# A four-layer diffusion backbone on one core: the first transfers in a fixed order, the latent stream first, and zero matmuls in idle places of TensorE

## The chip, the core and the metric

The kernel runs on one core of a Trainium2 chip. The engines of the core have their own instruction queues and run beside each other: TensorE (PE, with the loading of its weights shown apart as PEld), VectorE (DVE), ScalarE (ACT), GpSimd (POOL), and SyncE (SP), whose queue issues all transfers here. The metric is the time of one execution on the device in microseconds (us), as the median of several runs.

## The reference: what is computed

256 latent tokens and 256 context tokens, 1024 wide, go through four layers. Each layer has a token mixer (attention, pooling, retention, attention) and a SwiGLU feed-forward part (FFN), each behind an RMS norm that is modulated by a condition vector, with a gated residual. In the last layer the context stream has no output of its own.

```python
def pre_norm(xs, gain, shift, scale):
    return rmsnorm(xs, gain) * (1 + scale) + shift

def swiglu(h, w_gate, w_up, w_down):
    return (jax.nn.silu(h @ w_gate) * (h @ w_up)) @ w_down
...
    cond_lat = jax.nn.silu(c)[:, None, :]
    for i in range(DEPTH):
        sh_m, sc_m, g_m, sh_f, sc_f, g_f = jnp.split(cond_lat @ ada_w[i] + ada_b[i], 6, axis=-1)
        h_l = pre_norm(x_lat, norm_mix[i], sh_m, sc_m)
        ...                                  # the same for the context, with c_ctx
        x_lat = x_lat + g_m * y_l            # y_l: attention, pooling or retention
        x_lat = x_lat + g_f * swiglu(pre_norm(x_lat, norm_ffn[i], sh_f, sc_f),
                                     ffn_w_gate[i], ffn_w_up[i], ffn_w_down[i])
```

## The kernel before

**Data.** The activations stay on the chip, transposed: 128 partitions hold a block of features, KT = 8 such blocks (k) make the 1024, and the free axis holds 512 tokens, `STREAM[0]` the 256 latent and `STREAM[1]` the 256 context ones. Weights come from memory as 512 KB tiles `wall` (128x1024), modulation weights as tiles `adaw` of the same size. Products are exact to float32: each weight tile and each normed tile h is split into a rounded high part and the low rest (`w_prep`: ACT makes the high part with a CAST of 128x1024, DVE or POOL the low one with a subtraction of the same size; `norm2`: ACT and DVE or POOL make the parts of h), and three products are summed in PSUM, which has eight banks (`ps`, one 128x512 tile each).

**A norm.** `addsq` squares the stream's eight blocks (ACT) and sums them (DVE). `norm1` multiplies the sum by a column of ones on PE (128x1), takes the inverse root with a Newton iteration of some eight small DVE instructions, and puts it on a diagonal (two 128x128 DVE instructions). `norm2` spreads the diagonal over all partitions with a product against ones (two 128x128 on PE, "the spread" below), multiplies x by it and by the modulation (a DVE `SCALAR_TENSOR_TENSOR`), and writes h. In layers after the first this is called by `boundary`, which stands between two sub-layers: the latent stream is normed while the tail of the sub-layer before (`ctail`, on the context) still gives PE work, then the context, then the first products of the next sub-layer run. `boundary` in `pool` and in the FFN are two of its callers.

**The first layer.** `start` loads x, the first eight weight tiles and the modulation weights in pieces (`START`: 128, 128, 256 and 512 features, for scale and for shift), computes each piece's modulation on PE (32x128 matmuls, `ada_rows`), makes the h blocks that it allows, and runs the K and V products of the four token blocks (`kv`) as far as there is h. `consts` loads one table of small data (`small`: constants, rotary tables, the condition), and lets ACT compute silu of the condition.

**What sets the order.** The kernel is written as one sequence, recorded (`Recorder`), and laid out anew by a planner for the whole program: `schedule` tries priorities in several rounds, `attempt` gives each engine the ready instruction of the highest priority, with modelled costs, a bank of PSUM for each `ps` tile from its first to its last instruction, and data dependences as the only ties. So an edit in one place can move instructions in others. All instructions are emitted on one line (L550), so that rows of the profile name operation, tile and shape, not the place in the code.

Of the kernel before, what the change touches and what calls it, by code (L numbers as in the profile page):

```python
# [175 lines left out]
class Recorder:  # L176
# [23 lines left out]
    def record(self, eng, name, args, kw, calls=None):  # L200
# [59 lines left out]
        self.ops.append(op)  # L260

# [324 lines left out]
class Builder:  # L586
# [67 lines left out]

    def tr(self, out, in_):
        self.nc.tensor.transpose(out, in_, self.ident)
        self.clock += 0.109
# [98 lines left out]
    def consts(self):  # L756
        nc, cp, a = self.nc, self.cp, self.a
        sm = self.small = cp.tile([P, SM_END], F32, name="small", const=True)
        nc.sync.dma_start(sm, a["small"])
        x = self.xall = cp.tile([P, KT, 512], F32, name="x")  # L760
        self.x = [x[:, k, :] for k in range(KT)]
        self.ident = cp.tile([P, P], F32, name="ident", const=True)
# [10 lines left out]
        nc.scalar.activation(self.cond[:, :, 0:2], sm[:, SM_C:SM_END].rearrange("p (k c) -> p k c", c=2), AF.Silu)  # L773
        self.nsink = cp.tile([P, 32], F32, name="nsink", const=True)
# [43 lines left out]
    def norm1(self, s):  # L818
# [3 lines left out]
        for b in range(2):  # L822
            for i, t in enumerate(terms):
                self.mm(ps[:, b : b + 1], t[:, tb_cols(b)], self.inv_d, i == 0, i == len(terms) - 1)
        self.last[s] = []
# [7 lines left out]
    def norm2(self, s, A, B, ks=range(KT)):  # L833
# [3 lines left out]
        if ks[0] == 0:  # L837
            ps = self.ps()
            for b in range(2):
                self.mm(ps[:, tb_cols(b)], self.ones, self.dg[s][:, tb_cols(b)], True, True)  # L840
            self.rps[s] = ps
# [19 lines left out]
    def boundary(self, ctail, A, B, lhead, chead, ctx=True, fill=()):  # L861
# [139 lines left out]
    def ffn(self, l, ctail, ctx, bfill=(), fill=(), mid=None):  # L1001
# [52 lines left out]
        for half in range(2):  # L1054
            gs = []
            if half == 0:
# [12 lines left out]
                self.boundary(ctail, A, B, head(LAT), head(CTX), ctx, bfill)  # L1069
# [55 lines left out]
    def start(self, A, B, kv, setup):  # L1125
# [5 lines left out]
        def load_x(s):  # L1131
            for k in range(0, KT, 4):
                nc.sync.dma_start(self.xall[:, k : k + 4, STREAM[s]], self.a["xin"][s, :, k : k + 4, :])

        def load(c0, n, ci):
# [6 lines left out]
        load_x(0)  # L1142
        for i, p in enumerate(pieces):
            load(*p)
            if i == 1:
                load_x(1)
            if i % 2 and (p[0] + p[1]) % 256 == 0:
                self.w_dma()
        for s in range(2):
# [3 lines left out]
        gens = [kv(tb) for tb in range(4)]  # L1153
        for c0, n, ci in pieces:
# [19 lines left out]
            if ci == 0:  # L1174
                ks = range(c0 // P, (c0 + n) // P)
                for s in range(2):
                    self.norm2(s, A, B, ks)
                setup()
                for g in gens:
                    self.run(g, nq)  # L1180
        for g in gens:
            self.run(g)
# [53 lines left out]
    def attention(self, l, slot, ctail, need_ctx, bfill=(), fill=()):  # L1236
# [7 lines left out]
        self.adepth = 4  # L1244
        kvkeys = []
        for k in range(KT):
            for c in range(4):
                kvkeys.append(("attn_w_qkv", slot, ((k * P, P),), D + c * P))
# [29 lines left out]
        def kv(tb):  # L1278
            ps = self.ps()
            for k in range(KT):  # L1280
                self.mmR(ps, self.hx(k, tb_cols(tb)), self.blk(held[4 * k], 4), k == 0, k == KT - 1)
# [6 lines left out]
        def setup():  # L1288
            if not held:
                self.w_retire()  # L1290
                held.extend(self.take(kvkeys, True))
                KH.extend(self.slot(F32R) for _ in range(2))
# [8 lines left out]
        if l == 0:  # L1301
            self.start(A, B, kv, setup)
        else:
            self.boundary(ctail, A, B, head(0), head(1), True, bfill)
# [11 lines left out]
        def qgen(g):  # L1316
            qr = {}
            bs = self.take([("attn_w_qkv", slot, ((k * P, P),), g * 256 + c * P) for k in range(KT) for c in range(2)])
            for par in range(2):
                Q[g, par] = self.slot(F32R)  # L1320
# [20 lines left out]

            for tb in tbs:
# [685 lines left out]
```

## Time and profile before

| | us |
|---|---|
| median of 3 runs | 2198.64 (2198.44 to 2198.74) |
| profiled execution, its own time | 2198.0 |
| its span in the profile | 2196.2 |
| PE busy in the span | 2169.7 (99%) |
| weight loads on PE (PEld), beside its matmuls | 1826.2 (83%) |
| DVE busy | 1529.0 (70%) |
| ACT busy | 874.4 (40%) |
| POOL busy | 131.1 (6%) |

The profile is of one execution; 1.8 us of its time lie outside the span. PE has work nearly all the time, so the rows to read are those on the few stretches in which it has none, and on the clock it is granted: the clock column is 1.00 at the higher of its two levels (2.4 GHz) and 0.50 at the lower (1.2 GHz), and a mean of both lies between them.

### The profile page before, as it was taken

What the parts mean: (1) busy time and instruction counts of PE and PEld (TensorE: products, weight loads), DVE (VectorE), ACT (ScalarE), POOL (GpSimd) and SP (SyncE); (2) the same over time, 40 slices, a digit from 0 to 9 for tenths busy, and PEclk for the clock granted to TensorE, in tenths of its full rate; (3) what the DMA queues carried; (4) which work ended last, traced back from release to release, by engine and by line L of the source; (5) the groups of instructions that cost most, each with busy time, mean ns of one, the idle gap of its engine ahead of it and who ended that gap; (6) DMA issues with size and microseconds to landing.
All of it is one profiled execution on the core that took longest, in us unless ns stands there. A gap on an engine that the chain in (4) does not pass through costs nothing.

```text
span 2196.2 us, 29879 instructions
## 1 busy us (share of the span) xinstructions
PE 2169.7 (99%) x11378; PEld 1826.2 (83%) x11378; DVE 1529.0 (70%) x3075; ACT 874.4 (40%) x1529; POOL 131.1 (6%) x145
## 2 busy tenths in 40 slices
PE   8999999999999999999999999999999999999999
PEld 5787988888898888888888888889888888877888
DVE  5888867677598777766364554458677765898674
ACT  5587522223272222324332333335222223587552
POOL 2222000000010000000000000000000000441000
PEclk9999999999999999999999999999999999999999
DMA  9413545655235565532232232234456543125562
GB/s 380 164 36 105 183 145 171 227 165 185 75 131 196 182 232 180 169 119 82 73 97 90 77 96 77 82 110 159 158 163 220 172 143 116 49 87 192 163 203 85
DMA packets 88944, 315.27 MB, mean 144 GB/s; under 512 B 9824, under 2 KB 13024, under 8 KB 88800
## 3 DMA queue, kind: packets, MB, share of 16 engines
q1 hardware_dynamic: 88800, 313.36, 43.5%
q8 instruction: 89, 1.46, 0.3%
q14 instruction: 55, 0.45, 0.1%
HBM read 312.27 MB, written 1.05 MB: 143 GB/s over the span
## 4 chain that ended last, share of the span: by engine, by line
PE 95%; DVE 3%; DMA 1%; ACT 0%; issue 0%; SPq 0%; ACTq 0%; DVEq 0%
PE t L550 95%; DVE t L550 3%; ACT t L550 0%; DMA t<-wall 0%; DMA t<-xin 0%; ACT L550 0%; SPq L550 0%; ACTq L550 0%; DVEq L550 0%
## 5 line engine op out<-in xcount | busy, mean ns | idle before, releaser
L550 PE MATMUL t<-t,t 128*128 128x512 f32 (+5 forms) x11378 | 2169.7, 362 | 22.8 <-DVE t L550 18.7
L550 PEld LDWEIGHTS t<-t,t 128*128 128x128 f32 (+1 forms) x11378 | 1826.2, 185 | 366.0 <-issue 47.8
L550 DVE TENSOR_TENSOR t<-t,t 128x256 f32<-128x256 f32 (+7 forms) x1278 | 782.0, 642 | 395.2 <-ACT t L550 190.3
L550 ACT CAST t<-t 128x1024 fp32r<-128x1024 f32 (+3 forms) x646 | 526.5, 833 | 744.9 <-DVE t L550 343.3
L550 DVE SCALAR_TENSOR_TENSOR t<-t,t 128x1024 bf16<-128x1024 f32 (+5 forms) x472 | 400.4, 862 | 52.7 <-DMA t<-adaw 40.7
L550 ACT ACTIVATE t<-t 128x256 f32<-128x256 f32 (+4 forms) x357 | 160.7, 461 | 416.4 <-PE t L550 304.5
L550 DVE SCALAR_TENSOR_TENSOR t<-t,t,t 128x256 f32<-128x256 f32 (+2 forms) x500 | 229.4, 499 | 114.7 <-PE t L550 108.6
L550 POOL TENSOR_TENSOR t<-t,t 128x2 f32<-128x2 f32 (+5 forms) x124 | 127.5, 1038 | 1853.5 <-ACT t L550 1737.2
L550 ACT ACTIVATE t<-t,t 128x256 fp32r<-128x256 f32 (+2 forms) x180 | 89.2, 541 | 46.2 <-DVE t L550 45.4
L550 DVE TENSOR_REDUCE t<-t 128x1 f32<-128x512 f32 (+5 forms) x128 | 67.3, 551 | 16.0 <-PE t L550 14.9
L550 ACT COPY t<-t 128x256 f32<-128x256 f32 (+2 forms) x116 | 53.1, 469 | 56.4 <-PE t L550 52.5
L550 ACT ACTIVATE t<-t,t,t 128x512 f32<-128x512 f32 (+1 forms) x96 | 67.0, 706 | 19.7 <-DVE t L550 15.5
L550 DVE TENSOR_SCALAR t<-t 128x2 int32<-128x2 int32 (+4 forms) x84 | 16.1, 196 | 79.0 <-ACT t L550 71.6
L550 DVE TENSOR_SCALAR t<-t,t 128x512 f32<-128x512 f32 (+2 forms) x94 | 36.4, 419 | 1.0
L550 DVE DVE_READ_ACCUMULATOR t<-t,t 128x1 f32 x304 | 25.1, 82 | 0.0
L550 DVE COPY t<-t 128x512 f32<-128x512 f32 x32 | 21.8, 685 | 1.0 <-PE t L550 0.8
L550 ACT ACTIVATION_READ_ACCUMULATOR t<-t,t,t 128x1 f32 x96 | 19.3, 201 | 0.0
L550 DVE SCALAR_TENSOR_TENSOR t<-t 128x2 f32<-128x2 f32 (+1 forms) x94 | 15.6, 167 | 1.9
L550 ACT ACT_TABLE_LOAD x6 | 7.7, 1283 | 8.4 <-DVE t L550 5.7
L550 DVE TENSOR_TENSOR t<-t 128x2 f32<-128x2 f32 (+1 forms) x47 | 8.9, 192 | 0.9
L550 DVE RECIPROCAL t<-t 128x2 f32<-128x2 f32 (+1 forms) x40 | 6.4, 165 | 0.6
L550 ACT ACTIVATION_READ_ACCUMULATOR t<-t 128x1 f32 x32 | 6.3, 196 | 0.0
(9 smaller groups left out, 4.6 us busy)
## 6 DMA issues: line engine op xcount, KB each, us to landing
t<-wall SPq DMA_DIRECT2D x386, 512.0 KB, 3.7
t<-adaw SPq DMA_DIRECT2D x192, 512.0 KB, 4.6
t<-condw SPq DMA_DIRECT2D x6, 512.0 KB, 3.7
t<-xin SPq DMA_DIRECT2D x4, 512.0 KB, 5.9
t<-strips SPq DMA_DIRECT2D x4, 512.0 KB, 4.4
t<-pm SPq DMA_DIRECT2D x2, 512.0 KB, 4.1
out_dram<-t SPq DMA_DIRECT2D x8, 128.0 KB, 1.7
t<-small SPq DMA_DIRECT2D x1, 412.0 KB, 5.6
```

What stands on the lines that cost most here:

```text
L550: getattr(getattr(nc, op.eng), name)(*args, **kw)
```

## The change

- **Transfers.** `small` is loaded in three parts: condition first, then constants, the rotary tables last. A new `follow(a, b, ...)` records a tie between instructions, and the first ones of the queue are tied in this order: condition, two halves of the latent x, the first scale piece, constants, the first shift piece, a weight tile, the context x. The other pieces are loaded in groups.
- **First norm.** silu of the condition is ahead of the squares of the latent stream. Three of the eight latent squares are made by DVE. In the first layer the spread is copied from PSUM to a tile (`keep`) by ACT. The streams are interleaved as latent h, latent K and V, then context h, context K and V, in each piece; before, both streams' h came before the products.
- **Zeros.** `warm(count, n)` records matmuls of a bf16 tile of zeros with itself into a PSUM tile that nobody reads: 22 of 512 and 24 of 256 columns at the start, and 8 and 9 of 512 at two boundaries (`warm=True`): behind norm1 and behind the spread of the latent stream. The two callers are the FFN's boundary behind a mixer without context output (`not ctx`, layer 3) and the pooling layer's. The tie is only to what stands ahead of them; nothing waits for a zero.
- **Attention of layer 0.** `start` is called after the functions for q are defined; a part of `qgen` becomes `qfin`. `setup` makes the K and V tiles only when they are first needed.

```diff
+    def warm(self, count, n=512, after=None):
+        ps = self.ps()
+        for _ in range(count):
+            self.nc.tensor.matmul(
+                ps[:, 0:n], self.idle[:, 0:P], self.idle[:, 0:n], start=True, stop=True, skip_group_check=True
+            )
+            if after is not None:
+                self.nc.follow(after, self.nc.ops[-1])
...
-        nc.sync.dma_start(sm, a["small"])
+        for c0, c1 in ((SM_C, SM_END), (0, SM_PSC), (SM_PSC, SM_C)):
+            nc.sync.dma_start(sm[:, c0:c1], a["small"][:, c0:c1])
+            self.loads.append(nc.ops[-1])
...
+        nc.gpsimd.memset(self.idle, 0.0)
+        self.warm(22)
+        self.warm(24, 256)
...
+            if keep is not None:
+                nc.scalar.copy(keep[:, 0:256], ps[:, 0:256])
+                ps = keep
...
         self.norm1(0)
+        if warm:
+            self.warm(8, 512, self.normed)
         self.norm2(0, A, B)
+        if warm:
+            self.warm(9, 512, self.spread)
...
-                self.boundary(ctail, A, B, head(LAT), head(CTX), ctx, bfill)
+                self.boundary(ctail, A, B, head(LAT), head(CTX), ctx, bfill, not ctx)
...
+            for k in range(KT):
+                xs = self.x[k][:, LAT]
+                if k in (1, 3, 5):
+                    V.tensor_tensor(q[k], xs, xs, ALU.mult)
+                else:
+                    nc.scalar.activation(q[k], xs, AF.Square)
+                    if k == 0:
+                        nc.follow(self.silu, nc.ops[-1])
...
+        load_x(0)
+        load(*pieces[0])
+        line.append(self.loads[1])
+        load(*pieces[1])
+        self.w_dma()
+        line.append(nc.ops[-1])
+        load_x(1)
+        nc.follow(*line)
...
+        for i, (c0, n) in enumerate(START):
+            for ci in (2, 0):
+                modulation(c0, n, ci)
+            ks = range(c0 // P, (c0 + n) // P)
+            for s in range(2):
+                if i == 0 and s == 1:
+                    squares(1)
+                if i == 1 and s == 0:
+                    load_group(4)
+                self.norm2(s, A, B, ks, keep[s])
+                setup(False)
+                for g in streams[s]:
+                    self.run(g, n // P)
...
-        self.boundary(ctail, A, B, head(0), head(1), True, bfill)
+        self.boundary(ctail, A, B, head(0), head(1), True, bfill, True)
```

How the instructions stand on PE at the start of the program, before. The rows of 128x1 are norm1 of a stream, those of 32x128 a modulation block, those of 128x128 transposes and the spread, and the last is the first product (weights `t_274`, h `t_270`).

```order
L550 MATMUL t_167<-t_74,t_138 128x1
L550 MATMUL t_167<-t_74,t_156 128x1
...
L550 MATMUL t_191<-t_80,t_84 32x128 x8
L550 MATMUL t_210<-t_82,t_84 32x128 x8
...
L550 MATMUL t_231<-t_138,t_110 128x128
...
L550 MATMUL t_251<-t_87,t_84 32x128 x8
L550 MATMUL t_265<-t_74,t_174 128x1
...
L550 MATMUL t_288<-t_274,t_270 128x512
```

The same place after. `t_123` is the tile of zeros, `t_181` the latent norm1, `t_234` its spread, `t_283` the first product.

```order
L557 MATMUL t_134<-t_123 128x512
...
L557 MATMUL t_165<-t_79,t_74 32x128 x8
...
L557 MATMUL t_181<-t_84,t_148 128x1
...
L557 MATMUL t_186<-t_82,t_74 32x128 x8
...
L557 MATMUL t_234<-t_148,t_109 128x128 x2
...
L557 MATMUL t_242<-t_123 128x256
...
L557 MATMUL t_269<-t_89,t_74 32x128 x8
...
L557 MATMUL t_283<-t_219,t_275 128x512
```

Fourteen zeros now stand ahead of the first modulation block, one between it and norm1, seven more up to just behind the spread, and fourteen of 256 columns from there to the first product; the other ten of 256 columns stand among the first products. The context's norm1 (`t_265` of before) no longer stands ahead of the first product.

SP's queue from its first row on, before.

```order
L550 DMA t_72<-xin 128x4x256 x2
L550 DMA t_77<-small 128x824
L550 DMA t_72<-xin 128x4x256
L550 DMA t_80<-adaw 128x1024
L550 DMA t_82<-adaw 128x1024
L550 DMA t_72<-xin 128x4x256
L550 DMA t_87<-adaw 128x1024
L550 DMA t_89<-wall 128x1024
```

And after, with the rows of the last pieces of the first layer's modulation weights at the end (places 22 to 29).

```order
L557 DMA t_72<-small 128x16
L557 DMA t_76<-xin 128x4x256 x2
L557 DMA t_79<-adaw 128x1024
L557 DMA t_72<-small 128x256
L557 DMA t_82<-adaw 128x1024
L557 DMA t_86<-wall 128x1024
...
L557 DMA t_72<-small 128x552
...
L557 DMA t_132<-edge 128x64
L557 DMA t_179<-adaw 128x1024
L557 DMA t_193<-wall 128x1024
L557 DMA t_208<-adaw 128x1024
L557 DMA t_256<-adaw 128x1024
```

One weight tile (`t_86`) has moved ahead of the context x, `small` is in three pieces, and the last four modulation tiles of the first layer stand at places 26, 28, 29 and 33 of the queue, where before the last of them is at place 25.

PE at the boundary before the last FFN (layer 3), before: norm1 (`t_17921`), the spread (`t_17946`), and the first products of the FFN.

```order
L550 MATMUL t_17921<-t_74,t_138 128x1
L550 MATMUL t_17921<-t_74,t_17925 128x1
...
L550 MATMUL t_17946<-t_138,t_110 128x128 x2
L550 MATMUL t_17968<-t_17959,t_17775 128x512
L550 MATMUL t_17968<-t_17959,t_17790 128x256
L550 MATMUL t_17978<-t_17959,t_17620 128x512
```

And after.

```order
L557 MATMUL t_17992<-t_84,t_17994 128x1
...
L557 MATMUL t_18001<-t_123 128x512
...
L557 MATMUL t_18024<-t_148,t_109 128x128 x2
...
L557 MATMUL t_18031<-t_123 128x512
...
L557 MATMUL t_18056<-t_18044,t_17856 128x512
L557 MATMUL t_18056<-t_18044,t_17870 128x256
L557 MATMUL t_18062<-t_18044,t_17738 128x512
L557 MATMUL t_18062<-t_18044,t_17794 128x256
```

Eight zeros stand between norm1 and spread, nine between spread and first product, and four accumulations (`t_18056`, `t_18062`, `t_18067`, `t_18073`) now begin on the first h (`t_18044`).

The zeros recorded at the boundary of the pooling layer stand at two other places. On PE, after, around 630 us and in the attention of layer 3:

```order
L557 MATMUL t_6663<-t_249,t_109 128x128 x2
...
L557 MATMUL t_6669<-t_123 128x512
...
L557 MATMUL t_6685<-t_6455,t_5755 128x256
...
L557 MATMUL t_16749<-t_16368,t_16334 128x256
...
L557 MATMUL t_6669<-t_123 128x512
...
L557 MATMUL t_16854<-t_16622,t_16709 128x512
```

`t_6663` is the spread of the context at the boundary before the FFN of layer 1, with six zeros behind it; three more into the same tile `t_6669` stand some 5,800 rows later. Eight others (`t_6447`) stand before, behind the latent spread of the same boundary.

## Rows read from the trace of the kernel before

**Rows 1.** PE's waits, whole span: engine, line, released by: us, times, longest us

```profile
PE t L550 <- DVE t L550: 18.7, 10, 8.9
PE t L550 <- ACT t L550: 3.8, 6, 1.2
```

**Rows 2.** Windows: start:end length, busy us of each engine (instructions), clock, DMA share, GB/s

```profile
17.66:22.00 4.34, 4.29 (x33) 2.31 (x32) 3.94 (x18) 0.34 (x2) 0.00 (x0) 1.00 1.02 405
...
22.00:62.80 40.80, 40.62 (x282) 30.77 (x278) 25.83 (x65) 23.38 (x48) 22.51 (x16) 1.00 0.84 332
62.80:65.00 2.20, 0.07 (x1) 0.00 (x0) 2.20 (x22) 0.00 (x0) 0.00 (x0) 1.00 0.57 119
65.00:70.00 5.00, 4.95 (x32) 3.61 (x36) 4.43 (x13) 1.46 (x3) 1.43 (x2) 0.66 0.56 183
...
620.00:626.40 6.40, 5.68 (x33) 5.51 (x34) 4.84 (x23) 3.58 (x5) 0.00 (x0) 0.73 0.75 287
626.40:631.00 4.60, 2.39 (x17) 1.96 (x16) 4.60 (x14) 4.03 (x9) 0.73 (x1) 1.00 0.38 114
...
2006.50:2012.00 5.50, 5.45 (x16) 4.33 (x17) 5.42 (x11) 4.07 (x10) 3.41 (x4) 0.51 0.20 74
```

**Rows 3.** Timeline, start: start us, us, engine, line, operation, count [idle before <-releaser]

```profile
4.88 2.74 ACT L550 ACTIVATE t<-t 128x256 f32<-128x256 f32 x8 [2.87 <-DMA t<-xin]
...
7.64 1.28 ACT L550 ACT_TABLE_LOAD   x1
...
8.86 4.88 PE L550 MATMUL t<-t,t 128*128 128x1 f32 x43 [8.86 <-DVE t L550]
...
10.74 0.16 DVE L550 TENSOR_SCALAR t<-t 128x2 int32<-128x2 int32 x1 [0.52 <-PE t L550]
...
13.04 0.28 DVE L550 TENSOR_SCALAR t<-t,t 128x128 f32<-128x128 f32 x1
...
14.57 4.17 SPq L550 DMA_DIRECT2D t<-adaw  x4
...
16.12 0.51 ACT L550 ACTIVATE t<-t,t 128x256 fp32r<-128x256 f32 x1
```

**Rows 4.** PE by form, 17.6 to 18.4: count | busy us, mean ns

```profile
L550 PE MATMUL t<-t,t 128*128 128x512 f32 x2 | 1.2, 701 | 0.0
```

**Rows 5.** PE by form, 2012 to 2060: count | busy us, mean ns

```profile
L550 PE MATMUL t<-t,t 128*128 128x512 f32 x139 | 48.3, 394 | 0.0
L550 PE MATMUL t<-t,t 128*128 128x256 f32 x140 | 38.6, 278 | 0.0
```

**Rows 6.** PE's timeline, 619 to 642

```profile
628.86 0.97 PE L550 MATMUL t<-t,t 128*128 128x256 f32 x6 [1.24 <-ACT t L550]
```

**Rows 7.** Timeline, 1999 to 2012

```profile
2003.77 0.71 PE L550 MATMUL t<-t,t 128*128 128x128 f32 x4 [1.94 <-DVE t L550]
2003.82 1.22 DVE L550 TENSOR_TENSOR t<-t,t 128x1024 fp32r<-128x1024 f32 x1
...
2005.46 5.25 ACT L550 ACTIVATE t<-t,t 128x256 fp32r<-128x256 f32 x12 [0.35 <-DVE t L550]
...
2006.55 5.75 PE L550 MATMUL t<-t,t 128*128 128x512 f32 x16 [2.07 <-DVE t L550]
```

**Rows 8.** SP's timeline, 20 to 60: last modulation load of the first layer

```profile
28.43 0.33 SPq L550 DMA_DIRECT2D t<-adaw  x1
```

**Rows 9.** Timeline, 52 to 68: POOL, DVE and PE

```profile
53.38 9.22 POOL L550 TENSOR_TENSOR t<-t,t 128x256 fp32r<-128x256 f32 x6 [0.97 <-ACT t L550]
...
59.99 2.71 DVE L550 TENSOR_SCALAR t<-t 128x8 int32<-128x8 int32 x3
62.62 0.15 DVE L550 SCALAR_TENSOR_TENSOR t<-t 128x8 f32<-128x8 f32 x1
...
65.05 3.17 PE L550 MATMUL t<-t,t 128*128 128x128 f32 x19 [2.18 <-DVE t L550]
```

**Rows 10.** Page, costliest groups: a copy out of PSUM

```profile
L550 DVE COPY t<-t 128x512 f32<-128x512 f32 x32 | 21.8, 685 | 1.0 <-PE t L550 0.8
```

More of the change, by code (lines that the diff above doesn't have):

```diff
@@ L260, in record, with follow @@
         self.ops.append(op)
+    def follow(self, *ops):
+        for a, b in zip(ops, ops[1:]):
+            if a not in b.pred:
+                a.succ.append(b)
+                b.pred.append(a)
+                b.npred += 1
     def price(self, op):
@@ L831, in norm1, with norm2 @@
         self.dg[s] = dg
-    def norm2(self, s, A, B, ks=range(KT)):
+    def norm2(self, s, A, B, ks=range(KT), keep=None):
         nc = self.nc
@@ L859, in free_h, with boundary @@
         self.h = None
[L861 removed]
+    def boundary(self, ctail, A, B, lhead, chead, ctx=True, fill=(), warm=False):
         if ctail is not None:
@@ L1140, in load, with squares @@
                 nc.sync.dma_start(t, src.rearrange("p (k n) -> p k n", n=n))
[L1142 to L1149, printed above, removed]
+                line.append(nc.ops[-1])
+        def squares(s):
             for k in range(KT):
@@ L1173, in start, with load_group @@
             self.ada_rows(0, ci + c0 // 512, ps, c0 % 512 // P, nq)
[L1174 to L1181, printed above, removed]
+        load_x(0)
[3 more added lines that the diff above has]
+        self.w_dma()
+        line.append(nc.ops[-1])
+        load_x(1)
+        nc.follow(*line)
+        ndma = (0, 1, 2, 3, 4)
+        def load_group(i):
+            load(*pieces[2 * i])
+            load(*pieces[2 * i + 1])
+            while self.ndma < ndma[i]:
+                self.w_dma()
+        for i in range(1, 4):
+            load_group(i)
+        rowf = self.slot()
+        keep = [rowf[:, s, 0:256] for s in range(2)]
+        streams = [[kv(0), kv(1)], [kv(2), kv(3)]]
+        squares_lat()
+        for i, (c0, n) in enumerate(START):
[11 more added lines that the diff above has]
+                    self.run(g, n // P)
+        self.free(rowf)
+        setup()
+        for g in streams[0] + streams[1]:
             self.run(g)
@@ L1291, in setup @@
                 held.extend(self.take(kvkeys, True))
+            if late and not KH:
                 KH.extend(self.slot(F32R) for _ in range(2))
@@ L1314, in attention, with qfin @@
         Q = {}
[L1316 to L1320, printed above, removed]
+        def qfin(g, s, qr):
+            y = self.newton(ssq[:, g * 16 + s * 8 : g * 16 + s * 8 + 8], 8, 1.0 / 64)
+            nc.gpsimd.tensor_copy(rq[:, g, 2 * s : 2 * s + 2, :], y.rearrange("p (t h) -> p t h", t=2))
             def qtr(s):
@@ L1340, in qtr, with qgen @@
                     V.tensor_tensor(t[oth, :, c], src[own], t[own, :, c].bitcast(F32), ALU.subtract)
+            qtr(s)
+        def qgen(g):
+            qr = {}
+            bs = self.take([b for k in range(KT) for b in qkey(k, g)])
+            for par in range(2):
+                Q[g, par] = self.slot(F32R)
             for tb in tbs:
@@ L1356, in qgen @@
             yield
+        if l == 0:
+            self.start(A, B, kv, setup)
+        else:
+            self.boundary(ctail, A, B, head(0), head(1), True, bfill)
         self.run(qgen(0))
```

41 lines of the change are left out of this document (27 added, 14 removed).

## Prediction

> **What bounds the kernel now.** I read three views in this order. First the waits of PE, the TensorE: of a span of 2196.2 us it idles 18.7 us behind DVE in ten places, the longest (8.9) at the very start, and 3.8 us behind ACT in six [rows 1]. Everything else on PE is work, so the change can win only where PE is idle or where its clock is low. Then the windows by stage, which say where that is [rows 2]. From 22.0 to 62.8 us PE is busy 40.62 of 40.80 us at clock 1.00: nothing to win. Four places have something:
>
> (1) The start. PE's first instruction stands at 8.86, and the first product of the first layer (a 128x512 matmul) at 17.66 [rows 3, 4]. In the window 17.66 to 22.00 PE is busy 4.29 of 4.34 us, but a 128x512 takes 701 ns there against 394 ns later [rows 4, 5], so it runs at the lower level, although the clock column prints 1.00 (the profile has no clock record before 22). (2) 62.80 to 65.00: PE does 0.07 us of work, and in the five us after it the mean clock is 0.66 [rows 2]. (3) The FFN boundary of layer 1: 620 to 626.4 at clock 0.73, then 2.39 us of work in 4.60 [rows 2], the longer of two waits behind ACT [rows 6]. (4) The boundary of layer 3, 2000 to 2012: idle 1.94 and 2.07 us, both behind DVE [rows 7], then 5.5 us at clock 0.51 [rows 2].
>
> What the low clock costs in a window is its length times (1 - clock): (2) 5.0 x 0.34 = 1.7, (3) 6.4 x 0.27 = 1.7, (4) 5.5 x 0.49 = 2.7 us; in (1), where PE is saturated at half, 4.3 / 2 = 2.15 us.
>
> **Part by part: the price of a zero matmul.** No bf16 zero is in the trace. From 2012 to 2060 139 matmuls of 512 columns and 140 of 256 fill 48.0 us [rows 5], so 256 columns cost 48.0 / (278 + 140) = 0.115 us, 512 cost 0.23; at half clock 0.23 and 0.46. I take this for the zeros. A zero costs nothing while PE would wait longer than it takes; otherwise its full price.
>
> **Start, first product.** Now: the last squares wait for the second half of x; the two streams' squares and a second table load (1.28 us at 7.64) stand in ACT's queue; norm1 goes to PE at 8.86, newton begins on DVE at 10.74, the last diagonal is made at 13.04 + 0.28 = 13.32, the first h tile at 16.12 + 0.51, the first product at 17.66 [rows 3]. After: silu is ACT's first work, so one table load is gone, and three of the eight latent squares go to DVE. The loads of x keep their place but for 8 KB ahead of them, so the second half lands about as now, and norm1 stays near 8.6. What is gained lies behind it. The zeros have brought PE to full clock by then, so norm1 and the first modulation blocks, 8.86 to 10.74, take half: about -0.9. Newton and diagonals keep their 2.58 us: 12.3. The context stream's squares no longer stand ahead, but now there is a copy of the spread (ACT, behind one square, to 13.0); DVE makes the low half of the weight (1.22 as in [rows 7]) and one context sum of 0.42 ahead of the first h, which I put at 14.3; ACT ends it at 14.85. First product 15.0 against 17.66: -2.6. Bounds: 13.9 if DVE's 1.22 is fully beside the spread; 16.5 if norm1 is held by a modulation block whose weights land late (the queue delivers 512 KB every 1.28 us: four issues in 4.17 [rows 3]).
>
> **Start, clock.** With PE at full clock the stretch now between 17.66 and 22.0 loses its half: -2.15. What stands against it: ten 256-column zeros lie among the first products; if none falls into a gap they cost 10 x 0.115 = 1.15. I take 0.3, since they may stand only where products wait for h, and there are such waits while h is made one tile after the other.
>
> **Start, transfers.** The forced order and 276 KB of `small` put further back move the last modulation loads: now the last of them goes out at 28.43 [rows 8], as the 25th transfer or so; after, the last four stand at places 26, 28, 29 and 33. Of the eight places between, three are small pieces: five transfers at 1.28 us, so the last lands some 6.4 us later, while products come 4.75 us earlier. The K and V products that need it end with it; what PE has besides is the second group of q columns and one more modulation block, moved ahead of the K transposes. So 0 to 3 us; I take 0.5. Sum of the start: -2.6 - 2.15 + 0.3 + 0.5 = -3.95; bounds -1.2 - 2.15 + 1.15 + 3 = +0.8 and -3.75 - 2.15 = -5.9.
>
> **Idle at 62.8.** DVE's short chain for the norm of K runs into POOL: a DVE group of three 128x8 operations takes 2.71 us and ends at 62.70, just after POOL's six tensor operations end at 62.60, and PE waits 2.18 us [rows 9]. The change puts no zero there and leaves a 128x1024 POOL operation in the same chain. I keep idle and slow clock: 0.
>
> **Layer 1.** The zeros recorded at the pooling layer's boundary have come to stand at the next one, the FFN's: eight fall between the latent spread and its h, where PE waits for DVE and ACT; six fall behind the context spread, where the trace shows no gap; the last three come over a thousand us later, in the attention of layer 3. DVE is busy 4.60 of 4.60 us there [rows 2], so h comes when it comes. Gain: up to the clock's 1.7, but only if PE, not DVE, were late: bounds -2.0 and +1.4 (six zeros of 0.23). I take 0.
>
> **Layer 3.** Eight zeros stand between norm1 and spread, nine between spread and first product: 8 x 0.23 = 1.8 and 9 x 0.23 = 2.1 us, in idle of 1.94 and 2.07 [rows 7]. They fit. PE then stays at full clock, and 2.7 us come back if h keeps up: ACT makes 12 tiles in 5.25 us [rows 7], 0.44 each, eight of them h at 0.65; after, four accumulations are interleaved on each h, 4 x 512 and 3 x 256 columns or 11 x 0.115 = 1.27 us, so PE isn't starved. The idle itself remains, as DVE's order there, with 1.22 us of weight ahead of h, is the same. With 0.1 for overhang: -2.6, bounds -2.7 and -1.5 (h at 0.65 a tile governs).
>
> **Rest.** Splitting the q code into a function, the keys for K and V and the predecessors are no operations. Copies of the spread: two ACT copies of 128x256 that run beside PE's work, the first one counted above. Three DMAs for one of `small`: inside the transfers above.
>
> **Sum.** -3.95 + 0 + 0 - 2.6 = -6.55. The profiled run took 2198.0 (span 2196.2 and 1.8 around it); 2198.0 - 6.55 = 2191.45. The median of the runs stands 0.64 over the profiled one, so 2192.1.
>
> **Rivals.** (A) The idle at 62.8 goes too: with other places of q and POOL work DVE's chain no longer meets POOL. That gives a further 2.2 + 1.7 = 3.9: 2188.2. For it: the chain is written anew around it, and q products are moved there. Against it: POOL's large operation stands in the chain as before. The Trainium skill, "SBUF — State Buffer", section "Who interferes with whom", says that VectorE and GpSimd share a pair of ports and that whoever issues first keeps it for the whole instruction while the other blocks. The trace agrees: 2.71 us for three operations of a kind that takes some 0.15 us [rows 9]. By that rule the wait comes back wherever the two meet, and the time is 2192.1; only where they don't is it 2188.2.
>
> (B) Transfers bound the start: products that begin earlier run dry before the last modulation loads, which costs 3.0 in place of 0.5: 2194.6. For it: places 26 to 33 in a queue whose DMA share is 1.02 up to 22 us and 0.84 after it [rows 2]. Against: PE has q products and modulation work to fill with.
>
> (C) The zeros do not do what they are for: PE's clock stays low at the start and in layer 3 (too few of them, or holes between them). Then 2.15 and 2.6 are missing, with about 0.45 more at norm1: 2197.3.
>
> (D) Slower. The zeros of layer 1 are one accumulator, six written near 630 us and three near 1900: as it is one tile, one of eight PSUM banks is held all that time, through retention and FFN layers in which PE has hardly any idle time [rows 1]. If a product must wait for a bank, it waits about an eviction, 0.685 us [rows 10]. Ten such waits eat the gain, sixteen make the kernel measurably slower (11 / 0.685); twenty would give 2205.8. For it: PE there has no slack. Against it: the order was laid out with seven banks, and DVE and ACT have room to evict.
>
> **How the numbers follow.** Forecast 2192.1, chance 0.50, own range 2190 to 2194.5. (A) 0.20, (B) 0.17, (C) 0.08, (D) 0.05. A measurement of this kernel can tell 0.2%, 4.4 us, from no change: faster means under 2194.2, slower over 2203.0. Faster: 0.45 of the forecast, 0.20 of (A), 0.08 of (B), 0.73 in all. Same: 0.05, 0.09 of (B) and 0.07 of (C): 0.21. Slower: (D) and 0.01 of (C), 0.06. The range reaches from (A) with the start at its better bound, 2188.2 - 1.95 = 2186.2, to (C), 2197.3; outside are (D) and the tails.
>
> **What would show it.** Right: first 128x512 near 15 at some 400 ns; clock 1.00 all through 2006 to 2012, with about 4 us of zeros from 2002; PE idle of about 2 us still near 60 with DVE behind POOL; the clock at 620 to 626 not decisive, since h is late there. Wrong: idle behind DMA between 40 and 50 us (B); products over 600 ns at the start or after 2006 (C); new PE waits for ACT or DVE between 640 and 1900 (D); no idle near 60 (A).

## The result, and the profile after

The changed kernel took 2212.39 us as the median of 4 runs (2209.88 to 2213.06), the kernel before 2198.69 beside it (2198.44 to 2198.92): a ratio of 1.0061, 95% interval 1.0049 to 1.0073. The prediction was 2192.1, the result is 13.7 us slower than before. The profiled execution took 2212.0, its span is 2210.2.

PE's waits of after, whole span (engine, line, released by: us, times, longest us; [rows 1] of before):

```profile
PE t L557 <- DVE t L557: 8.9, 7, 5.3
PE t L557 <- ACT t L557: 6.3, 7, 2.2
PE t L557 <- POOL t L557: 2.3, 1, 2.3
PE t L557 <- DMA t<-adaw: 1.1, 1, 1.1
PE t L557 <- issue: 0.2, 1, 0.2
```

PE waits less than before (18.8 us against 22.5) and yet the time is longer. The start is the reason that the totals mislead: the zeros, counted as work, fill it. In the trace 75 of the 80 zeros are recorded, as one group of the page of after:

```profile
L557 PE MATMUL t<-t 128*128 128x512 bf16 (+1 forms) x75 | 19.5, 397 | 2.7 <-POOL t L557 2.3
```

What is new above all is the one wait of 5.3 us behind DVE. The windows of after say where time is lost (columns as in [rows 2]):

```profile
7.20:17.14 9.94, 8.66 (x86) 5.70 (x86) 6.57 (x26) 4.33 (x12) 0.00 (x0) 0.83 1.04 391
...
45.90:51.30 5.40, 0.07 (x1) 0.00 (x0) 5.37 (x5) 0.10 (x1) 5.24 (x3) 0.71 0.82 329
51.30:55.00 3.70, 3.69 (x20) 2.88 (x21) 0.80 (x3) 0.00 (x0) 0.00 (x0) 0.50 0.44 124
...
62.80:70.00 7.20, 7.20 (x44) 6.40 (x43) 5.53 (x21) 5.18 (x15) 2.27 (x4) 1.00 0.43 147
85.00:95.00 10.00, 8.44 (x47) 6.74 (x46) 9.43 (x37) 9.42 (x23) 1.15 (x5) 0.88 0.17 63
630.00:641.00 11.00, 10.62 (x81) 9.33 (x81) 9.98 (x36) 8.51 (x18) 1.03 (x2) 1.00 0.75 271
...
2010.00:2020.00 10.00, 8.55 (x53) 5.80 (x53) 9.01 (x25) 8.30 (x14) 0.00 (x0) 1.00 0.53 169
2019.80:2025.00 5.20, 5.18 (x29) 4.45 (x30) 4.63 (x10) 4.19 (x10) 2.73 (x4) 1.00 0.21 80
```

From 45.9 to 51.3 PE does 0.07 us of work while DVE and POOL are both busy nearly all the time, and then the clock is 0.50 for 3.7 us: some 7.2 us in one place where before had none [rows 2]. The stretch at 62.8, idle before, is full now. From 85 to 95 PE is short of work: its longest wait there, 1.29 us, is behind ACT, which with DVE makes the softmax of the first heads (ACT 9.42 of 10, DVE 9.43); before, the same ten microseconds held 10.00 of PE work at clock 1.00.

To place the loss, the work of PE without the zeros is summed from each trace (each matmul at one price by its columns), and the times are compared at which the same sum is done. Rows from 226.7 on are the first 128x1 matmul of a norm, and the end of the span. Each column after the first is a profiled execution minus before. The kernels do the work of the first layer in different orders, so the rows down to 90.2 depend on the price: with other prices by columns they move by up to some 1.6 us (45.9, at the edge of the idle, by more), the rows from 226.7 on not at all.

| before, us | after | x1 | x6 | e1 | e7 |
|---|---|---|---|---|---|
| 21.3 | -0.7 | -0.5 | -2.4 | -1.4 | +0.5 |
| 45.9 | -0.5 | -0.2 | -1.9 | -0.9 | +1.1 |
| 53.8 | +6.9 | +0.2 | -1.5 | -0.5 | +2.7 |
| 73.5 | +2.7 | -4.0 | -5.7 | -4.7 | -1.5 |
| 90.2 | +8.3 | +1.6 | -0.1 | -5.0 | +1.0 |
| 226.7 (FFN, layer 0) | +10.2 | +3.4 | +2.1 | -2.1 | +3.7 |
| 986.7 (FFN, layer 2) | +11.7 | +5.2 | +3.1 | -2.5 | +2.5 |
| 2196.2 (end) | +14.0 | +8.8 | +3.6 | -6.3 | +4.9 |

So ten of the fourteen microseconds are lost in the first layer: 7.4 at 46 us, 4.2 won back where before idled at 62.8, 5.6 lost again by 90 us, and 1.9 up to 226.7 (how the last two divide depends on the price). Later come 1.2 at the boundaries from 593 to 637, some 2 in the attention of layer 3 (waits of 1.62 and 2.24 us at 1923 and 1986), and in this one execution some 3 in the last FFN (below, e4); the boundary of layer 3 gives 2 back.

What happens at 46 us, in the timeline of after (start us, us, engine, ...):

```profile
40.11 8.81 DVE L557 TENSOR_TENSOR t<-t,t 128x1024 fp32r<-128x1024 f32 x4
41.02 10.13 POOL L557 TENSOR_TENSOR t<-t,t 128x1024 fp32r<-128x1024 f32 x4 [0.20 <-ACT t L557]
...
48.85 2.33 DVE L557 TENSOR_SCALAR t<-t 128x32 f32<-128x32 f32 x1
51.10 0.16 DVE L557 TENSOR_REDUCE t<-t 128x4 f32<-128x16 f32 x1
...
51.31 4.95 PE L557 MATMUL t<-t,t 128*32 128x256 f32 x29 [5.34 <-DVE t L557]
```

The first row groups one large operation with three small ones; DVE by form, 40 to 51.2 (count | busy us, mean ns), takes them apart:

```profile
L557 DVE TENSOR_TENSOR t<-t,t 128x64 f32<-128x64 f32 x2 | 4.8, 2390 | 0.0
L557 DVE TENSOR_TENSOR t<-t,t 128x128 f32<-128x128 f32 x1 | 2.5, 2480 | 0.0
L557 DVE TENSOR_SCALAR t<-t 128x32 f32<-128x32 f32 x1 | 2.3, 2332 | 0.0
L557 DVE TENSOR_TENSOR t<-t,t 128x1024 fp32r<-128x1024 f32 x1 | 1.8, 1782 | 0.0
```

The four small operations are the three products of one of the two sets of rotary tables and the negated sink: setup work that reads the third part of `small`. Before, DVE did the same kind of work at the start, beside an idle POOL (before, DVE by form, 7 to 11 us):

```profile
L550 DVE TENSOR_TENSOR t<-t,t 128x64 f32<-128x64 f32 x4 | 0.7, 218 | 0.0
L550 DVE TENSOR_TENSOR t<-t,t 128x128 f32<-128x128 f32 x2 | 0.6, 284 | 0.0
...
L550 DVE TENSOR_SCALAR t<-t 128x32 f32<-128x32 f32 x1 | 0.2, 174 | 0.0
```

What takes 0.17 to 0.28 us there takes 2.33 to 2.48 in after, about the length of one of POOL's four 128x1024 subtractions (10.13 us). A reduction that PE waits for stands behind them in DVE's queue and comes at 51.10; PE's wait ends when it is done. They are so late because the third part of `small` is issued at 23.01 (SP's timeline of after, 19 to 34) and lands 9.7 us later by the page's list of issues (KB each, us to landing):

```profile
23.01 0.33 SPq L557 DMA_DIRECT2D t<-small  x1
```

```profile
t<-small SPq DMA_DIRECT2D x1, 276.0 KB, 9.7
```

### The profile page after: what moved, and what is told of

Read it like the earlier page. It is cut to its first block, busy times and chain, and to the rows that moved or that the text cites. A ratio compares the mean times of both kernels' runs of the same rounds, so it can differ in the third digit from the quotient of the medians.

```text
span 2210.2 us, 30060 instructions
## 1 busy us (share of the span) xinstructions
PE 2186.9 (99%) x11453; PEld 1830.5 (83%) x11458; DVE 1540.3 (70%) x3078; ACT 874.7 (40%) x1527; POOL 132.8 (6%) x146
## 4 chain that ended last, share of the span: by engine, by line
PE 93%; DVE 4%; ACT 2%; DMA 1%; issue 0%; SPq 0%; POOL 0%; DVEq 0%; ACTq 0%; POOLq 0%
PE t L557 93%; DVE t L557 4%; ACT t L557 2%; DMA t<-adaw 0%; DMA t<-wall 0%; SPq L557 0%; ACT L557 0%; POOL t L557 0%; DVEq L557 0%; ACTq L557 0%; POOLq L557 0%
## 5 line engine op out<-in xcount | busy, mean ns | idle before, releaser
L557 PE MATMUL t<-t,t 128*128 128x512 f32 (+4 forms) x11378 | 2170.4, 361 | 17.0 <-DVE t L557 8.9
L557 DVE TENSOR_TENSOR t<-t,t 128x1024 fp32r<-128x1024 f32 (+9 forms) x1278 | 781.8, 643 | 402.0 <-ACT t L557 192.9
L557 ACT CAST t<-t 128x1024 fp32r<-128x1024 f32 (+4 forms) x646 | 526.4, 834 | 744.5 <-DVE t L557 346.6
L557 DVE SCALAR_TENSOR_TENSOR t<-t,t 128x1024 f32<-128x1024 f32 (+5 forms) x471 | 403.8, 873 | 56.5 <-DMA t<-adaw 47.2
L557 POOL TENSOR_TENSOR t<-t,t 128x1024 fp32r<-128x1024 f32 (+5 forms) x124 | 128.4, 1043 | 1869.3 <-ACT t L557 1752.1
L557 ACT COPY t<-t 128x256 f32<-128x256 f32 (+2 forms) x118 | 53.8, 468 | 65.6 <-PE t L557 61.3
L557 PE MATMUL t<-t 128*128 128x512 bf16 (+1 forms) x75 | 19.5, 397 | 2.7 <-POOL t L557 2.3
L557 DVE SCALAR_TENSOR_TENSOR t<-t 128x2 f32<-128x2 f32 (+2 forms) x95 | 19.3, 204 | 2.4
L557 PEld LDWEIGHTS <-t 128*128 128x128 bf16 x80 | 8.3, 111 | 10.9 <-issue 5.5
L557 DVE TENSOR_TENSOR t<-t 128x2 f32<-128x2 f32 (+2 forms) x50 | 8.8, 177 | 4.2 <-DMA t<-xin 3.1
```

What stands on the lines that cost most here:

```text
L557: getattr(getattr(nc, op.eng), name)(*args, **kw)
```

## The experiments

Each kernel ran beside the kernel before on the same chip, whose medians there were 2198.03 to 2198.52, with more scatter between runs than above (2194.8 to 2205.6). Theory: the late rotary work beside POOL makes the loss. Rivals: the address of the zeros' tile, the PSUM bank that the layer 1 zeros hold, the zeros themselves, or the modulation loads put further back. In the edits `op.mark` is a label that `warm`, `w_prep` or the table code writes on its instructions; dropping or moving marked instructions behind `schedule` leaves the planned order of all others as in after.

### x1: the four table operations ahead of the weight's low part

```diff
+def ahead(order):   # DVE: the marked table operations go ahead of the "low" that stands before them
+    ...
+    return rest[:i] + moved + rest[i:]
...
-        order = b.nc.schedule()
+        order = ahead(b.nc.schedule())
```

> The changed kernel with its planned order, but for one move on DVE: the weight's 128x1024 subtraction near 40 us stands behind the four small instructions on the rotary and sink tables instead of ahead of them. Theory (DVE is blocked by POOL): in the changed kernel those four take 2.33 to 2.48 us each, one beside each of POOL's four 128x1024 subtractions; ahead of POOL's first, at 41.0, they take some 0.25 each, DVE reaches its reduction near 45 instead of 51.1, PE's idle of 5.34 at 46 and the low clock behind it (6.8 us at half, 3.4) go: 2212.4 - 8.7 = 2203.7, at most 2206 if the one large subtraction now waits for POOL and is late for its products. Rival (the modulation loads, put further back, hold PE at 46): the idle stays, 2211 to 2213.

Measured: 2203.53 (10 runs), ratio 1.0024 (1.0015 to 1.0034). The unmoved order, with only the zeros' tile elsewhere (e4, below), ran on the same chip at 2211.95: 8.4 us between the medians come from four operations in another place of one queue. In the profiles it is 6.8 (after) or 5.6 (e4) at 226.7; the runs of one kernel scatter by as much as these differ. SP's queue is that of after, so the modulation loads are not what holds PE at 46. The expected 8.7 counted the whole low clock behind the idle, 6.8 us; 3.1 of them lie in the idle itself. Timeline and window of x1:

```profile
33.70 20.58 PE L558 MATMUL t<-t,t 128*128 128x512 f32 x148
...
40.39 1.11 DVE L558 TENSOR_TENSOR t<-t,t 128x64 f32<-128x64 f32 x3
41.27 10.61 POOL L558 TENSOR_TENSOR t<-t,t 128x1024 fp32r<-128x1024 f32 x4 [0.20 <-ACT t L558]
41.42 2.37 DVE L558 TENSOR_SCALAR t<-t 128x32 f32<-128x32 f32 x1
...
45.94 0.17 DVE L558 TENSOR_REDUCE t<-t 128x4 f32<-128x16 f32 x1 [1.02 <-PE t L558]
```

```profile
45.90:51.30 5.40, 5.40 (x50) 4.86 (x49) 5.25 (x4) 0.39 (x1) 5.40 (x3) 1.00 1.04 413
```

Three of the four run before POOL starts (1.11 us together), only the fourth is held. The reduction comes at 45.94 instead of 51.10, and PE works without a hole and at clock 1.00 where after idled. The reduction itself takes 0.17 us in the middle of POOL's four, so not every DVE operation is held.

### x6: POOL's four subtractions on DVE

```diff
+def swap(order):
+    lows = [op for op in order if op.eng == "gpsimd" and op.mark == "low"]
+    for op in lows[:4]:
+        op.eng = "vector"
+    return order
...
-        order = b.nc.schedule()
+        order = swap(b.nc.schedule())
```

> The changed kernel with its planned order, POOL's first four 128x1024 subtractions (41 to 51 us) given to DVE at the places that they have in the order. Theory (POOL blocks DVE's four small instructions): these take 0.2 to 0.3 us each though the tables come as late as in the changed kernel; DVE has 4 x 1.22 = 4.9 us more work, but saves 8.7 of waiting, so that its reduction comes near 46 instead of 51.1 (two of the four stand behind it), PE's idle falls from 5.3 to under 1.5 and the clock mostly stays: 2204 to 2208. Rival (the tables themselves come too late, or DVE has too much to do): more work on DVE makes it later: 2213 to 2217.

Measured: 2202.64 (9 runs) against before's 2198.06, ratio 1.0028 (1.0018 to 1.0037). DVE has four times 1.2 us more to do, in the same order, and yet the kernel is only 4.6 us over before where after is 13.7 over: 9.1 us back, slightly more than expected. DVE by form in x6, 40 to 51.2:

```profile
L558 DVE TENSOR_TENSOR t<-t,t 128x1024 fp32r<-128x1024 f32 x5 | 6.6, 1328 | 0.0
...
L558 DVE TENSOR_TENSOR t<-t,t 128x64 f32<-128x64 f32 x2 | 0.4, 210 | 0.0
L558 DVE TENSOR_TENSOR t<-t,t 128x128 f32<-128x128 f32 x1 | 0.3, 277 | 0.0
...
L558 DVE TENSOR_SCALAR t<-t 128x32 f32<-128x32 f32 x1 | 0.2, 167 | 0.0
```

With POOL silent the table operations, some 30 us later than in before, take 0.17 to 0.28 us again. So lateness alone does not lengthen them; lateness beside POOL's long operations does. The rule that the prediction drew from the Trainium skill ("SBUF — State Buffer", "Who interferes with whom": whoever issues first keeps the shared ports for its whole instruction) agrees with both runs, and I used it too narrowly: a short DVE operation that is held takes about as long as the long one of POOL beside it (2.33 to 2.48 us, POOL's four 10.13).

### e1: `small` in two parts

```diff
-        for c0, c1 in ((SM_C, SM_END), (0, SM_PSC), (SM_PSC, SM_C)):
+        for c0, c1 in ((SM_C, SM_END), (0, SM_C)):
```

> The changed kernel with `small` in two parts in place of three: condition first, then constants and rotary tables together ahead of the second modulation piece. The whole program is laid out anew by the planner. Theory (the late tables put DVE's rotary instructions beside POOL's 128x1024): they stand ahead of the first products again, none takes over 1 us, PE's idle of 5.3 us near 46 and the low clock behind it are gone: 2212.4 - 8.7 + 0.7 for the transfers = 2204, give or take 3 for the new layout. Rival (the modulation loads are what comes late): 276 KB more ahead of them, 0.7 us later: 2212 to 2214 with the idle there.

Measured: **2192.56** (2191.05 to 2195.59, 10 runs), ratio 0.9976 (0.9965 to 0.9986): faster than both kernels. The tables now come with the constants, and DVE makes them at the start (timeline of e1):

```profile
9.95 0.30 DVE L557 TENSOR_SCALAR t<-t 128x64 f32<-128x64 f32 x2 [0.64 <-DMA t<-small]
10.19 0.76 DVE L557 TENSOR_TENSOR t<-t,t 128x128 f32<-128x128 f32 x4
...
10.87 0.23 DVE L557 TENSOR_SCALAR t<-t 128x32 f32<-128x32 f32 x2
...
15.39 1.95 PE L557 MATMUL t<-t,t 128*128 128x512 f32 x20
...
25.66 28.51 PE L557 MATMUL t<-t,t 128*128 128x512 f32 x196 [0.30 <-ACT t L557]
```

It came some 11 us below what I had expected. The edit is planned anew, and in the new plan the shortage at 90 us is gone too, though 2.9 us go between 90.2 and 226.7 in the table. From 85 to 95 e1's ACT is as busy as after's, but PE finds other products:

```profile
85.00:95.00 10.00, 9.70 (x78) 8.05 (x81) 9.64 (x31) 9.79 (x26) 0.39 (x2) 1.00 0.64 238
```

x1 still has that shortage (+5.6 between 73.5 and 90.2 in the table, as in after). That the filler, the q products, was used up earlier in after is argued from these counts (47 matmuls against 78), not shown by a run of its own. So e1 shows that the forecast time can be reached with early tables, but not how much of its 19.8 us below after is the tables and how much the new plan; for that x1 and x6 stand.

### b3: the kernel before with `small` in three parts

```diff
-        nc.sync.dma_start(sm, a["small"])
+        for c0, c1 in ((SM_C, SM_END), (0, SM_PSC), (SM_PSC, SM_C)):
+            nc.sync.dma_start(sm[:, c0:c1], a["small"][:, c0:c1])
```

> The kernel before with `small` loaded in the changed kernel's three parts and nothing else of the change. The planner now puts the part with the rotary tables at place 27 of SP's queue, and DVE's rotary instructions 40 rows later, to some 40 us. Theory (late tables beside POOL's 128x1024 subtractions): several of them take about 2.4 us, PE waits for DVE, or K's norm comes later: 3 to 9 us slower than before, 2201 to 2207. Rival (only together with the forced order and the other streams): 2198, give or take 1.

Measured: 2200.20 (10 runs), ratio 1.0014 (1.0005 to 1.0023): 2.1 us lost, less than the 3 to 9 expected, more than the rival's 1. The tables are late here too, but the plan puts most of them into gaps of POOL (timeline of b3):

```profile
49.00 2.41 POOL L550 TENSOR_TENSOR t<-t,t 128x1024 fp32r<-128x1024 f32 x1 [0.39 <-ACT t L550]
49.27 3.22 DVE L550 TENSOR_TENSOR t<-t,t 128x1024 fp32r<-128x1024 f32 x1
...
52.54 7.68 PE L550 MATMUL t<-t,t 128*128 128x512 f32 x41 [0.89 <-DVE t L550]
...
54.38 0.88 DVE L550 TENSOR_SCALAR t<-t 128x64 f32<-128x64 f32 x2
55.19 1.04 DVE L550 TENSOR_TENSOR t<-t,t 128x128 f32<-128x128 f32 x6
```

So the split alone costs something. That the amount depends on which POOL operation the plan sets beside the tables is what the two plans, this one and after's, suggest.

### x2, x3, x4: the zeros of one place left out, order otherwise as in after

```diff
-        order = b.nc.schedule()
+        order = [op for op in b.nc.schedule() if op.mark not in ("pool",)]   # x3: "start", x4: "last"
```

> The changed kernel with its planned order, the 17 zeros recorded at the pooling layer's boundary left out of PE's queue. Theory (six of them lie where PE has no gap): 6 x 0.213 = 1.3 us less near 640 us and 0.6 near 1900: 2210.5. What the eight ahead of h held up, the clock, falls again at the boundary before the FFN of layer 1: up to +1.7, then 2212. Rival (a PSUM bank held from 640 to 1900 us makes products wait): several us less, spread over 700 to 1900 us: under 2208.

> The changed kernel with its planned order, the 46 zeros of the start left out. Theory (zeros keep the clock up but also take PE time among the first products): 128x512 products at some 430 to 570 ns until 22 us, +2.2, norm1 and the modulation at half clock, +0.5, against 1 to 2 us of zeros between products that go: 2212.4 + 1 = 2213.4. Rival (the zeros do nothing for the clock that the kernel's own work doesn't): 1 to 2 us less, 2211.

> The changed kernel with its planned order, the 17 zeros before the last FFN left out. Theory (they keep PE's clock up there): two idle stretches of some 2 us come back near 2016 and the clock falls to half for some 5.5 us behind them: +2.0 to +2.7, 2214.4 to 2215.1. Rival (h governs the first products, the zeros bring nothing): 2212.

Measured: x2 2210.22 (1.0034 to 1.0067), x3 2214.91 (1.0051 to 1.0088), x4 2211.18 (1.0047 to 1.0078). The intervals are some 7 to 8 us wide, and x4's median went the rival's way (2212 expected if the zeros bring nothing), so the profiles have to tell. x2: after's difference to before goes from +11.7 at 986.7 us of before to +11.5 at 1866.9, and x2's from +10.3 to +10.2, so nothing is lost while the layer 1 zeros hold a bank. The clock, which was expected to fall at the FFN's boundary of layer 1, stays at 1.00 in x2 too. x3: without the start's zeros the first product comes at 17.37, the first six of 512 columns take 680 ns each in the mean where after's take 425, and at 226.7 x3 trails after by 2.5. x4: both idles of [rows 7] are back, and the products behind them are slow:

```profile
2017.52 0.90 PE L558 MATMUL t<-t,t 128*128 128x128 f32 x4 [1.94 <-DVE t L558]
2020.30 5.07 PE L558 MATMUL t<-t,t 128*128 128x512 f32 x15 [1.88 <-DVE t L558]
```

### b1, b2: the zeros of one place added to the kernel before

```diff
+        self.idle = self.stp.tile([P, 512], BF16, tag="idle", name="idle", bufs=1, const=True)
+        nc.gpsimd.memset(self.idle, 0.0)
...                                     # b1: warm(8, 512, ...) and warm(9, 512, ...) at the boundary of layer 3
+        self.warm(22)                   # b2: these two
+        self.warm(24, 256)
```

> The kernel before with the 17 zeros before the last FFN and nothing else of the change; but for some twenty instructions there the planner leaves the order as it was. Theory: clock 1.00 from 2006 to 2012 instead of 0.51, -2.0 to -2.7: 2196. Rival (zeros overhang, h governs): 2198.5.

> The kernel before with the 46 zeros at the start and nothing else of the change (loads, silu and streams as before). Theory (the zeros bring PE to full clock before the first products): norm1 and modulation half a us to 0.9 faster, the products from 17.7 to 22 at full clock, -2.2, against up to 1 us of zeros in the way: 2196.5. Rival (the clock falls again between the zeros, or they stand in the way): 2198 to 2199.5.

Measured: b1 2196.62 (11 runs, 0.9982 to 1.0002), b2 2196.43 (11 runs, 0.9982 to 1.0000), against 2198.03. Both come near what was expected and lean to a gain of 1.5 us that the scatter doesn't quite settle. In b1's profile the boundary of layer 3 is full and at clock 1.00, where before had 7.38 of PE work in the same twelve microseconds at 0.72:

```profile
2000.00:2012.00 12.00, 11.10 (x59) 7.70 (x60) 10.68 (x27) 8.96 (x17) 3.09 (x4) 1.00 0.30 93
```

### e8, e7: e1 without the start's zeros; e1 without the layer 1 zeros, tile of zeros elsewhere

```diff
-        order = b.nc.schedule()
+        order = [op for op in b.nc.schedule() if op.mark != "start"]          # e8
...
-        self.idle = cp.tile([P, 512], BF16, name="idle", const=True)
+        self.idle = self.stp.tile([P, 512], BF16, tag="idle", name="idle", bufs=1, const=True)   # e7
-        self.boundary(ctail, A, B, head(0), head(1), True, bfill, True)
+        self.boundary(ctail, A, B, head(0), head(1), True, bfill)                                # e7
```

> The changed kernel with `small` in two parts, its planned order, the 46 zeros of the start left out. Theory (zeros pay by the clock): as where they were left out of the changed kernel itself (+2.5 there): 2192.6 + 2 = 2194.6. Rival (they only fill): 2192 or less.

> The changed kernel with `small` in two parts, without the pooling layer's 17 zeros, the tile of zeros behind the slots; laid out anew. Theory: as with two parts alone, less the six zeros that lie where PE has no gap: 2192.6 - 1 = 2191.6. Rival (they cost nothing there, the layout decides): 2190 to 2196 by the layout.

Measured: e8 2197.69 (10 runs, 0.9985 to 1.0004), 5.1 above e1 and 3 above what was expected. Of the 5.1, only 2.1 stand at 226.7 in the profiles, which is what the start's zeros are worth in e1's order as far as these two executions tell. Most of the rest comes in the last FFN, where e8 was profiled with products of 399 ns and e1 of 391 (below); e8's runs fall into two groups, four at 2193.9 to 2195.0 and six at 2197.7 to 2200.6. e7 2200.14 (11 runs, 1.0005 to 1.0023): outside the theory and the rival, 7.6 above e1, although each of its edits alone was harmless or better in after's order (e4, x2). It is planned anew, and its profile has new small waits at 55, 73 and 1919 to 1930 us. The plan decides more than the edit here; which of its choices does was not found.

### e4: the tile of zeros in another pool, the order as in after

```diff
-        self.idle = cp.tile([P, 512], BF16, name="idle", const=True)
+        self.idle = self.stp.tile([P, 512], BF16, tag="idle", name="idle", bufs=1, const=True)
```

> The changed kernel, every instruction in the same order; the 1 KB per partition of zeros lies behind the weight and h slots instead of ahead of them, so that the slots begin 1 KB lower, at the address of the kernel before. Theory (place in SBUF): the products of the last FFN, where the moving operand is two pieces of 256 columns, take 231.5 ns a step again instead of 236.0, and those of 256 columns 115.6 instead of 117.3; over 528 pairs 3.3 us: 2209.1. Rival (the slower step comes of the order, or of the zeros): no difference, 2212.4, 236 ns.

Measured: 2211.95 (4 runs, 1.0038 to 1.0079), as after. The reason for trying was that in after's profile a 128x512 product of the last FFN takes longer than the 394 ns of [rows 5] (after, PE by form, 2040 to 2190; e4, then x1, 2030 to 2180):

```profile
L557 PE MATMUL t<-t,t 128*128 128x512 f32 x426 | 150.5, 399 | 0.0
```

```profile
L557 PE MATMUL t<-t,t 128*128 128x512 f32 x434 | 150.4, 391 | 0.0
```

```profile
L558 PE MATMUL t<-t,t 128*128 128x512 f32 x434 | 150.5, 391 | 0.0
```

x1 keeps the address of after and has 391, so the address is not the cause.

## Why the prediction was wrong

**The step that failed** is one clause under "Rest": "Three DMAs for one of `small`: inside the transfers above." I priced the split as transfers and not by who reads them. The last part holds the rotary tables; at place 22 of the queue (counted from 0) it lands near 33 us, DVE's table work runs 30 us later than before, and there POOL has its long subtractions. The rows to see it were ahead of the prediction: the order shows the 552 columns of `small` far down SP's queue, and [rows 9] show what a short DVE operation costs beside POOL. I used them for the idle at 62.8 alone. Price: 7.4 us in the profile at 46 us; x1 gives 8.4 and x6 9.1 back between the medians. Of the sign "idle behind DMA between 40 and 50 us" the idle came, but behind DVE; rival B fell, as PE's one wait for a transfer in after, 1.1 us, comes ahead of the first product, and x1 has the same loads and no idle at 46.

**First product, 15.0: right in size, in part by luck, and not in every execution.** The profiled execution of after shows 17.14. The same order in e4 gives 15.21, and e1 15.39:

```profile
15.21 1.76 PE L557 MATMUL t<-t,t 128*128 128x512 f32 x7
```

In e4 norm1 came at 9.29 where the sum had 8.6, and newton and diagonals took 2.04 us (10.38 to 12.42) where it had 2.58: two errors that nearly cancel. Of the 1.9 us between e4 and after 0.45 come from norm1, at 9.74 in after; the rest is PE's clock: 0.83 in after's window from 7.2 to 17.14, so that norm1 and what follows take longer, and 1.00 in the same window of x2, where the first product stands at 15.32:

```profile
7.20:17.14 9.94, 9.65 (x95) 6.34 (x95) 7.90 (x30) 5.79 (x16) 0.00 (x0) 1.00 1.02 386
```

Just before, PE had idled behind a modulation tile: 1.06 us in after and 0.82 in x1, where the clock fell; 0.68 in x4, 0.63 in x6, 0.35 in e4 and none in x2, where it stayed, all with the same order on PE there. But e1, in another order, idled 1.39 and kept the clock, so I can't name the cause. My upper bound, 16.5 for a late modulation block, had its wait but not the clock, and did not reach this execution.

**Start, clock: right.** From the first product on, at 17.14, products run at the higher level, as the term of -2.15 had it; without the zeros (x3) they do not. The net of the start is smaller, since zeros and modulation blocks now stand among the products: -0.7 in after's profile at 21.3, -2.4 in x6, against -3.95.

**Idle at 62.8, taken as 0: rival A came true.** In the profile of after and in all that came from it the idle is gone: 4.2 us gained between 53.8 and 73.5 in the table, against A's 3.9. DVE's 128x8 operations begin at 68.0 in after, where POOL is silent from 66.0 to 69.6, and the first two take 0.38 us together. But 5.6 us are lost by 90 us in the softmax, and from 53.8 to 226.7 after loses 3.3 net. The prediction had no term for that stretch, where PE was full before; that a plan which uses its filler early owes it later is my reading, not shown. This is the second part of the miss: x1, without the table wait, is still 5.0 above before, and loses 3.2 net in the same stretch. A third lies in the attention of layer 3, which the prediction left out as well: 2.1 us in after, and 5.4 in x1, whose clock fell behind both waits there (0.57 from 1919 to 1923 and from 1984 to 1988). Which part of the change makes these two was not tested.

**Layer 1: taken as 0, inside the bounds.** After loses 1.2 us from 592.9 to 637.3, where the eight zeros stand, and x2, without them, 0.5; the other kernels of this order lose 0.6 to 1.9, so the difference is hardly clear of the scatter. From 637.3 to 986.7, where the six stand that the bound of 1.4 priced, after and x2 both lose 0.3: the six cost nothing that shows. The clock is 1.00 at this boundary in after (630 to 641) and without the zeros in x2, so the zeros had nothing to bring back; why it fell in before and not here was not tested.

**Layer 3: right in after's profile, -2.6 predicted, but not in every execution.** There the clock is 1.00 throughout, with zeros in the idle; by the sums of work after gains 2.0 to 2.3, b1 2.5, and x4, without the zeros, 0.25. In e4, with the same order on PE, the clock still fell in the stretch of the zeros (the same ten microseconds about the boundary as the window 2010 to 2020 of after, which shows 1.00), and 1.2 us were gained:

```profile
2009.40:2019.40 10.00, 8.59 (x48) 5.81 (x48) 8.15 (x24) 7.40 (x13) 0.00 (x0) 0.83 0.53 181
```

Of the ten profiles with these zeros the clock stays at 1.00 in four (after, x6, e1, b1) and falls in six, behind norm1 and with zeros running; there it is low for 3.4 us in place of before's 6.8, and high again when the first products come, 0.6 to 0.8 us later behind norm1 than in the four. So in these six the zeros shorten the stretch at low clock and do not remove it.

**Rival C fell as a whole** (the zeros do raise the clock: x3, x4, b1), though in some executions it fell again among them, as above. **Rival D fell**: nothing is lost between 700 and 1850 us; its "slower" came true by another way. The forecast's time was met by e1, 2192.56, but with the tables early and by another sum (A's gain, and no net loss from 53.8 to 226.7), so that it lies so near is luck.

## What to carry to other kernels

When a load is split or put later, list its readers, not only its bytes: the instructions that read it move with it, and their price is that of the place where they land. In these runs a VectorE TENSOR_TENSOR or TENSOR_SCALAR of 32 to 128 columns beside a 128x1024 GpSimd subtraction took 2.3 to 2.5 us in place of 0.2 to 0.3 (a TENSOR_REDUCE was not held), and what stood behind it in VectorE's queue came later too; so such setup work belongs where GpSimd is silent. With a planner that lays the whole program out anew, compare edits in a fixed order first (drop or move marked instructions behind the planner), or its own spread (7.6 us between e1 and e7) hides what the edit is worth.

## What the runs showed that I had not expected

- The 128x512 products of the last FFN have two lengths, 391 to 394 ns and 399 ns, in the same order and at the same addresses; after, x2 and e8 were profiled at 399, the others at 391 to 394. Over some 500 products that is 3 to 4 us of a single execution, about the scatter between runs. The cause stays open.
- The clock fell once more in some executions of one order and not in others, with zeros running in between: at the start (0.83 in after and x1, 1.00 in x2; the fall costs some 1.5 us at the first product) and at the boundary of layer 3 (0.83 in e4, 1.00 in after).
- A 128x32 operation with one input (`TENSOR_SCALAR`, 2.33 us against 0.17) is held by POOL just like those with two.
